# Four convolution channel tiles instead of two during prompt attention, softmax scaling on ScalarE, low parts on VectorE, first steps reordered

## The chip, the cores and the metric

The kernel runs on one core of one Trainium2 chip. The metric is device time in microseconds (us), lower is better. Times of a kernel are medians of several executions; the trace comes from one more execution, taken with the hardware profiler.

Engines are named as in the profile: PE is TensorE (matmuls and transposes), PEld its weight loads, DVE is VectorE, ACT is ScalarE, POOL is GpSimd, SP is SyncE, which issues most transfers. L1108 is line 1108 of the kernel before.

## What is computed

One layer of a hybrid model in fp32, for a prompt of 512 tokens and 8 single-token samples together (520 columns, model width 1024):

```
z = rms_norm(x) @ w_in                 -> u2, q, k/v of three branches, gates
u = u2[:, :1024] * sigmoid(u2[:, 1024:])
c = conv1d(u, 31 taps per channel)     -> layer_norm -> silu -> @ w_conv_pw
a = sparse attention of 16 heads: compressed keys, selected blocks, window;
    each branch: softmax(q.k - slope * distance), times a gate, times v
x = x + (sigmoid(g_conv)*c + sigmoid(g_attn)*a) @ w_out
y = rms_norm(x + relu(rms_norm(x) @ w_up)^2 @ w_down)
```

The prompt attends to itself. The samples attend to paged caches of 2,048 positions in device memory, fetched by gathers. For the prompt, the selected blocks are all blocks, so it has two full branches and a short compressed one.

## The kernel before

**Layout.** Activations lie transposed, channels on the 128 partitions and the 520 columns along the free axis, so the model width is 8 channel tiles. A dense product (`dense`, L433 to L435) takes three fp32r matmuls per 128x128 weight tile, because each fp32 operand is split into a high part (a cast) and a low part (the difference): `hH*wh + hL*wh + hH*wl`. For every 128 output channels `wload` fetches the weights in two halves `wraw` (128x512), casts each on ACT to `wh` (L411) and subtracts for `wl` (L412). Two such `wh`/`wl` pairs exist. L412 runs on `LOW[0]`, which is POOL from the start and `LOW2` from the sample stage on; the third to sixth weight tile and the two large products at the end use DVE.

**Stages.** The order on each engine comes from a planner that simulates the program with priorities, except for the first normalization, whose order is the string `NORDER`.

1. Start (0 to 75 us). `norm1` normalizes five row tiles of x: `q` squares and sums a row tile on ACT, `s` turns sums into factors on DVE and ACT, `m` multiplies by the factor and the gain on DVE (L338), `t` transposes on PE (L346), casts to `hH` on ACT (L348) and subtracts for `hL` on DVE (L349). Then the first q tiles are projected. `small_loads` issues small constants on SP; `small_prep` transposes `vr` and the convolution weights `cwr` with PE (L308). `build_k` makes high and low parts of a head group's keys in one half of the partitions, and a DMA on ACT's queue copies them to the other half (L624).
2. Prompt attention (75 to 455 us). `attend` runs 4 head groups, each with two pairs of heads, each pair with two full branches: 16 units. A unit scores 4 query tiles of two heads (PE L688), adds distances and takes a minimum (DVE L651), exponentiates (ACT L655), scales the probabilities (L739 on DVE for query tiles 1 and 2, L741 on POOL for 0 and 3), transposes them (PE L750), copies them out of PSUM into `pt` (L753, one head on ACT, one on DVE) and multiplies by v (PE L755). Projections of the next group, pooling of the compressed cache (POOL gathers, L317) and the first convolution tiles fill in around it.
3. Convolution. `u_proj` computes the gated channel tile `u` (two buffers, `U1`); `conv_taps` then runs 31 taps per tile on DVE, a first one (L1101) and 30 more (L1108), each reading `u` shifted by one column and the sum `y`. `UP1` and `Y1` = 2 tiles have their `u` and `y` in memory of the prompt stage; the other six need memory that comes free after it. `U_EARLY` says behind which score matmul the PE work of an early `u` is queued, `V_AT` behind which score operation the first later tile's first tap is queued.
4. Sample stage (455 to 660 us). For 10 columns of work, cache rows are gathered, transposed on PE, copied by ACT, scored, exponentiated and weighted (L936 to L953), while the other six convolution tiles run on DVE and gate projections on PE.
5. Transition (660 to 725 us): sample results, convolution norm (L1179, L1182), activation (L1212 to L1219), its split (L1225, L1226), `gate_conv` projections.
6. Merge and output product (725 to 815 us), then the two large products (to 1195 us).

`after(ins)` wraps `tc.issue_after(ins)`. This queues the wrapped instructions behind `ins`, but only those that run on the same engine as `ins`, and it adds no wait between engines.

Of the kernel before, what the change touches and what calls it, by code (L numbers as in the profile page):

```python
# [17 lines left out]
P = 128  # L18
# [14 lines left out]
TL_S = True  # L33
KTS_B, SG_B, U1, Y1, UP1 = 5, 6, 2, 2, 2
SC_D = (1, 2)
PS1 = {"pss": 2, "pst": 2, "pso": 1, "psp": 1}
# [3 lines left out]
SORDER = (8, 9, 0, 1, 2, 3, 4, 5, 6, 7)  # L40
LOW2 = "gpsimd"
CG_B, QK_B = 4, 2
CONV_D = (0, 1, 2, 3, 4, 5, 6, 7)
CONV_S, W_V2 = (), 20
PT_A = (0,)
RT_E = lambda nc: nc.gpsimd
# [9 lines left out]
U_AT, V_AT = 108, 121  # L56
U_EARLY = (32, 48, 0, 0)
POOL_P, PROJ_D = True, False
# [6 lines left out]
SQ_D, WARM, EARLY = (), 20, 2  # L65
NORDER = "q0 s01 q1 m0 s12 m1 t0 t1 q2 q4 q3 s25 m4 m2 t4 m3 t2 t3"
PACK = 5000
# [63 lines left out]
def hybrid_layer(ctx: ExitStack, tc: tile.TileContext, I, C, O):  # L131
# [14 lines left out]
    def f32(ap):  # L146
        return ap.bitcast(F32)
# [124 lines left out]

    def small_loads():
        nc.sync.dma_start(wp, I["cmp_w"][0])
        cw_ = I["cmp_w"]
        for s in range(2):
            nc.sync.dma_start(wq[:, s], bass.AP(tensor=cw_.tensor, offset=cw_.offset + 32 * s, ap=[[0, 32], [8, 4], [1, 8]]))
        nc.sync.dma_start(wqb, bass.AP(tensor=cw_.tensor, offset=cw_.offset + 32, ap=[[0, 8], [2, 16], [1, 2]]))
        for r in range(2):
            nc.sync.dma_start(pos2[:, :, r], I["cmp_pos"][0])  # L280
        for s in range(2):
            nc.sync.dma_start(w1bd[64 * s:64 * s + 64, :, 64 * s:64 * s + 64], I["cmp_w1"][0].rearrange("j d e -> d j e"))
            nc.sync.dma_start(w2bd[64 * s:64 * s + 64, :, 64 * s:64 * s + 64], I["cmp_w2"][0].rearrange("j e f -> e j f"))
        nc.sync.dma_start(dist, C["dist"])
        for i, n in enumerate(("ln2_g", "conv_b", "conv_ln_g", "conv_ln_b")):
            nc.sync.dma_start(vr[8 * i:8 * i + 8], I[n][0].rearrange("(k p) -> k p", p=P))
        nc.sync.dma_start(cwr, I["conv_w"][0])

# [32 lines left out]
    def norm1():  # L321
# [14 lines left out]
        def scale(j):  # L336
            n = P if j < 4 else NB
            dve.scalar_tensor_tensor(xts[j][:n], xts[j][:n], rs[:n, 0, j:j + 1], g1b[:n], op0=OP.mult, op1=OP.mult)  # L338

# [15 lines left out]
        for op in NORDER.split():  # L355
            a = int(op[1])
            if op[0] == "q":
                squares(a)
            elif op[0] == "s":
                stats(slice(a, int(op[2])))  # L360
            elif op[0] == "m":
                scale(a)
            else:
                last = turn(a)
# [14 lines left out]
        return last  # L379

    hH = hp.tile([P, KD, T], F32R, name="hH", tag="H")
    hL = hp.tile([P, KD, T], F32R, name="hL", tag="L")
# [20 lines left out]

    def wload(w, pieces, r0=0, low=None):
        raws = early.pop(pieces[0][0], None) or wfetch(w, pieces, r0)
        o = sum(n for c, n in pieces)
        wh = wts.tile([P, KD, P], F32R, name="wh")
        wl = wts.tile([P, KD, P], F32R, name="wl")
        for h, raw in enumerate(raws):
            a, b = wh[:, KD // 2 * h:KD // 2 * h + KD // 2, :o], wl[:, KD // 2 * h:KD // 2 * h + KD // 2, :o]  # L410
            act.copy(a, raw[:, :, :o])  # L411
            (low or (dve if 2 <= len(loaded) < LOW_D else LOW[0])).tensor_tensor(b, raw[:, :, :o], f32(a), op=OP.subtract)  # L412
        loaded.append(wh)
        return wh, wl

    def after(ins):
        return tc.issue_after(ins.ins) if ins else nullcontext()
# [196 lines left out]
    def build_k(g, r, ap):  # L614
        kt = KV[g][0]
        w = ap.tile([P, 2, NP_ + 32], F32R, name="rt", bufs=RT_B)
        t = RT[g, "k", r] = w[:, :, 32:]
        RT[g, "ck", r] = w
        if r == 1 and g > 0:
            add_ck(g)  # L620
        a, o = 64 * r, 64 - 64 * r
        act.copy(t[a:a + 64, 0], kt[a:a + 64, :NP_])
        dve.tensor_sub(t[a:a + 64, 1], kt[a:a + 64, :NP_], f32(t[a:a + 64, 0]))
        DUP_E(nc).dma_start(f32(t[o:o + 64]), f32(t[a:a + 64]))  # L624

# [3 lines left out]
    def attend(g, ap):  # L629
# [10 lines left out]
        for pr in range(2):  # L640
# [24 lines left out]
            for r in (0, 1, -1):  # L665
# [69 lines left out]
                for e in range(2):  # L735
                    for i in range(4):
                        ph = phs[e][i]
                        if i in SC_D:
                            dve.tensor_scalar(ph, ph, rr[:, e, i:i + 1], None, op0=OP.mult)  # L739
                        else:  # L740
                            pool.tensor_scalar(ph, ph, rr[:, e, i:i + 1], 1.0, op0=OP.mult, op1=OP.mult)  # L741
                for js in ((0,), (1,), (2, 3)):
# [344 lines left out]
    def conv_taps(ks, share):  # L1087
        prev = None
        for k in ks:
# [9 lines left out]
            else:  # L1099
                with after(HV[V_AT] if k == max(UP1, ks[0]) and V_AT else prev):  # L1100
                    dve.tensor_scalar(yk, u[:, 0:NP_], cwT[:, k, 0:1], cbv[:, k:k + 1], op0=OP.mult, op1=OP.add)  # L1101
            for w in range(1, CW):
# [229 lines left out]
    with tc.manual_schedule():  # L1332
        last = norm1()
    ready = [wload(w_in, [(C_Q + P * t, P)]) for t in range(2)]
    small_loads()
# [308 lines left out]
```

## Time and profile before

| | |
|---|---|
| median of 3 runs | 1199.42 us (1198.84 to 1204.34) |
| profiled execution, its own time | 1196.95 us |
| span in the trace, first to last instruction | 1195.18 us, 1.77 us less than its own time |
| mean granted TensorE clock | 0.981 of full speed |
| busy in the span | PE 94%, PEld 86%, DVE 65%, ACT 47%, POOL 32% |

Busy means that an instruction is in the engine. Matmuls overlap, and their ends are modelled, so PE can be 100% busy below its peak rate. An engine's idle time in a stretch is the length of the stretch minus its busy time. The granted clock is 1.0 at 2.4 GHz and 0.5 at 1.2 GHz. Times in rows count from the start of the span.

### The profile page before, as it was taken

The numbers are of one execution on the slowest core, as the hardware profiler recorded it, in microseconds if no ns is written. First come the engines' busy times: TensorE is split into PE (matmuls) and PEld (weight loads), VectorE is DVE, ScalarE is ACT, GpSimd is POOL, SyncE is SP. The second block draws the span as 40 slices with busy tenths as digits, with TensorE's granted clock in tenths as the row PEclk, the third lists the DMA queues.
The fourth block names the chain that finished last, engine by engine and source line by source line (L and its number), as shares of the span: only waits on it lengthen the run. The fifth ranks groups of instructions, "written<-read, shape, count | busy, mean of one in ns | idle before, by whom it ended". The sixth has DMA issues, their size and how long they took to land.

```text
span 1195.2 us, 24820 instructions
## 1 busy us (share of the span) xinstructions
PE 1126.9 (94%) x9755; PEld 1025.3 (86%) x9755; DVE 773.2 (65%) x1712; ACT 557.1 (47%) x1404; POOL 385.2 (32%) x378
## 2 busy tenths in 40 slices
PE   6899999998999999989889979999999999999996
PEld 6787976876776888878777769999999999999996
DVE  6442566595977868999998886456543443443476
ACT  5453477545667544445444454344431441431454
POOL 2435637545652333545553334440000000000012
PEclk8899999999999999999999889999999999999999
DMA  6645654564468417867774233333333333333354
GB/s 180 196 137 165 191 168 118 158 175 150 116 185 298 133 38 274 279 241 250 252 253 169 64 105 108 89 89 107 89 96 100 89 89 89 95 99 90 89 164 138
DMA packets 189037, 176.78 MB, mean 148 GB/s; under 512 B 35309, under 2 KB 171053, under 8 KB 183656
## 3 DMA queue, kind: packets, MB, share of 16 engines
q1 hardware_dynamic: 172472, 96.54, 28.5%
q0 software_dynamic: 15296, 76.55, 18.2%
q10 hardware_dynamic: 1152, 2.10, 0.8%
q8 instruction: 77, 1.26, 0.4%
q14 instruction: 40, 0.33, 0.1%
HBM read 167.58 MB, written 14.80 MB: 153 GB/s over the span
## 4 chain that ended last, share of the span: by engine, by line
PE 71%; DVE 20%; DMA 4%; issue 2%; SPq 1%; ACT 1%; POOL 1%; DVEq 0%; POOLq 0%; ACTq 0%
PE psd L433 18%; PE psd L435 17%; PE psd L434 17%; DVE y L1108 13%; PE pss L688 4%; PE pst L750 3%; PE pso L755 3%; PE psp L783 2%; DMA wraw<-in_w_in_dram 1%; DMA cg<-in_cache_cmp_kv_dram,gic 1%; DVE tq L943 1%; DVE y L1212 1%; DMA rt<-rt 1%; PE pso L729 1%; PE psp L790 1%
## 5 line engine op out<-in xcount | busy, mean ns | idle before, releaser
L411 ACT CAST wh<-wraw 128x512 fp32r<-128x512 f32 x282 | 161.7, 617 | 266.9 <-PE psd L434 201.8
L433 PE MATMUL psd<-hH,wh 128*128 128x256 f32 (+2 forms) x848 | 248.3, 295 | 2.2 <-ACT gc L1249 1.3
L435 PE MATMUL psd<-hH,wl 128*128 128x256 f32 (+2 forms) x848 | 247.1, 294 | 0.1
L434 PE MATMUL psd<-hL,wh 128*128 128x256 f32 (+2 forms) x848 | 245.7, 291 | 0.0
L412 POOL TENSOR_TENSOR wl<-wraw,wh 128x512 fp32r<-128x512 f32 x130 | 180.7, 1409 | 199.5 <-ACT wh L411 188.3
L1108 DVE SCALAR_TENSOR_TENSOR y<-u,cwT,y 128x512 f32<-128x512 f32 x240 | 221.7, 924 | 6.0
L433 PEld LDWEIGHTS psd<-hH,wh 128*128 128x128 f32 (+1 forms) x848 | 160.7, 190 | 7.6 <-issue 2.5
L435 PEld LDWEIGHTS psd<-hH,wl 128*128 128x128 f32 (+1 forms) x848 | 160.4, 190 | 4.3 <-issue 2.8
L434 PEld LDWEIGHTS psd<-hL,wh 128*128 128x128 f32 (+1 forms) x848 | 160.8, 190 | 1.8 <-issue 0.7
L433 PE MATMUL psd<-xgH,wh 128*128 128x264 f32 (+1 forms) x512 | 144.8, 283 | 0.0
L434 PE MATMUL psd<-aT,wh 128*128 128x264 f32 (+1 forms) x512 | 144.7, 283 | 0.0
L433 PE MATMUL psd<-aT,wh 128*128 128x264 f32 (+1 forms) x512 | 144.7, 283 | 0.0
L435 PE MATMUL psd<-aT,wl 128*128 128x264 f32 (+1 forms) x512 | 144.7, 283 | 0.0
L435 PE MATMUL psd<-xgH,wl 128*128 128x264 f32 (+1 forms) x512 | 144.5, 282 | 0.0
L412 DVE TENSOR_TENSOR wl<-wraw,wh 128x512 fp32r<-128x512 f32 x152 | 103.9, 723 | 62.5 <-ACT wh L411 59.3
L434 PE MATMUL psd<-xgL,wh 128*128 128x264 f32 (+1 forms) x512 | 144.2, 282 | 0.0
L1583 POOL TENSOR_TENSOR attnT<-attnT,gfb 128x512 f32<-128x512 f32 (+1 forms) x8 | 10.5, 1331 | 368.7 <-DVE sqd L1578 368.7
L434 PEld LDWEIGHTS psd<-xgL,wh 128*128 128x128 f32 x512 | 96.6, 189 | 0.0
L655 ACT ACTIVATE pp<-pp,st 128x256 f32<-128x256 f32 (+3 forms) x128 | 71.6, 559 | 53.7 <-DVE st L651 52.1
L435 PEld LDWEIGHTS psd<-xgH,wl 128*128 128x128 f32 x512 | 96.5, 188 | 0.0
L433 PEld LDWEIGHTS psd<-aT,wh 128*128 128x128 f32 x512 | 96.3, 188 | 0.1
L433 PEld LDWEIGHTS psd<-xgH,wh 128*128 128x128 f32 x512 | 96.3, 188 | 0.0
(378 smaller groups left out, 2326.3 us busy)
## 6 DMA issues: line engine op xcount, KB each, us to landing
wraw<-in_w_in_dram SPq DMA_DIRECT2D x88, 256.0 KB
wraw<-in_w_down_dram SPq DMA_DIRECT2D x80, 256.0 KB
wraw<-in_w_up_dram SPq DMA_DIRECT2D x64, 256.0 KB
sg<-in_state_win_kv_dram POOLq DMA_DIRECT2D x8, 1024.0 KB
out_dram<-in_state_win_kv_dram SPq DMA_DIRECT2D x8, 1022.0 KB
wraw<-in_w_in_dram SPq DMA_DIRECT2D x32, 128.0 KB
wraw<-in_w_conv_pw_dram SPq DMA_DIRECT2D x16, 256.0 KB
wraw<-in_w_out_dram SPq DMA_DIRECT2D x16, 256.0 KB
```

The costliest lines, as they stand in the source:

```text
L411: act.copy(a, raw[:, :, :o])
L412: (low or (dve if 2 <= len(loaded) < LOW_D else LOW[0])).tensor_tensor(b, raw[:, :, :o], f32(a), op=OP.subtract)
L433: pe.matmul(ps[:n], wh[:, k, :n], aH[:, k, c], start=(k == 0), stop=False)
L434: pe.matmul(ps[:n], wh[:, k, :n], aL[:, k, c], start=False, stop=False)
L435: end = pe.matmul(ps[:n], wl[:, k, :n], aH[:, k, c], start=False, stop=(k == KD - 1))
L655: act.activation(ph, ph, AF.Exp, scale=-1.0, bias=st[:, 0, e, i:i + 1], accum_out=st[:, 1, e, i:i + 1])
L688: hpe = pe.matmul(ps, rq[:, e, P * i:P * i + P], kk[:, l, 32 - xi:32 + nk], start=(l == 0), stop=(l == 1))
L729: packed([lambda i=i, e=e: pe.matmul(po[64 * e:64 * e + 64, P * i:P * i + P], VcZ[:, i], pt[:, e], start=False, stop=True, skip_group_chec ...
L750: pe.transpose(ps[:, o:o + P], phs[e][i][:, P * j:P * j + P], ident)
L755: packed([lambda j=j, e=e: pe.matmul(po[64 * e:64 * e + 64, P * j:], vt[:, j, r], pts[e][:, off[j]:off[j] + P * (4 - j)], start=(r == 0 an ...
L783: packed([lambda r=r, j=j, i=i: pe.matmul(po[32 * i:32 * i + 32, j], wpa[:, 2 * rh + r, j], gs[i][:, r, 256 * j:256 * j + 256], start=(rh ...
L1108: prev = dve.scalar_tensor_tensor(yk, u[:, w:w + NP_], cwT[:, k, w:w + 1], yk, op0=OP.mult, op1=OP.add)
```

## The change

- `UP1` and `Y1` go from 2 to 4: four channel tiles have their `u` and `y` in the prompt stage, and `U_EARLY` queues the PE work of the third and fourth behind score matmuls 56 and 74 of 128. `U1` stays 2.
- The probabilities of all four query tiles are scaled on ACT (an activation `Copy` with a per-partition scale) instead of on DVE and POOL, and both `pt` copies run on ACT (`PT_A`).
- A tile's first tap runs on ACT instead of DVE.
- `LOW2` becomes DVE: from the sample stage on, L412 leaves POOL.
- Start: both sums before the factors (`q0 q1 s02`), tile 0 and 1 multiplied one after the other; `after(scaled[1])` around L412 of the first two weight tiles; `vr` and `cwr` are loaded first among the small loads; for head group 0, ACT and DVE write the second half of the keys instead of a DMA.
- The scratch memory for descriptors of POOL's transfers is set to 8192 bytes per partition, half of the default.

```diff
-KTS_B, SG_B, U1, Y1, UP1 = 5, 6, 2, 2, 2
-SC_D = (1, 2)
+KTS_B, SG_B, U1, Y1, UP1 = 5, 6, 2, 4, 4
-LOW2 = "gpsimd"
+LOW2 = "vector"
-PT_A = (0,)
+PT_A = (0, 1)
-U_EARLY = (32, 48, 0, 0)
+U_EARLY = (32, 48, 56, 74)
-NORDER = "q0 s01 q1 m0 s12 m1 t0 t1 q2 q4 q3 s25 m4 m2 t4 m3 t2 t3"
+NORDER = "q0 q1 s02 m0 m1 t0 t1 q2 q4 q3 s25 m4 m2 t4 m3 t2 t3"
...
     def small_loads():
+        nc.sync.dma_start(cwr, I["conv_w"][0])
+        for i, n in enumerate(("ln2_g", "conv_b", "conv_ln_g", "conv_ln_b")):
+            nc.sync.dma_start(vr[8 * i:8 * i + 8], I[n][0].rearrange("(k p) -> k p", p=P))
         nc.sync.dma_start(wp, I["cmp_w"][0])
...
-        for i, n in enumerate(("ln2_g", "conv_b", "conv_ln_g", "conv_ln_b")):
-            nc.sync.dma_start(vr[8 * i:8 * i + 8], I[n][0].rearrange("(k p) -> k p", p=P))
-        nc.sync.dma_start(cwr, I["conv_w"][0])
...
-                scale(a)
+                scaled.append(scale(a))
...
-    def wload(w, pieces, r0=0, low=None):
+    def wload(w, pieces, r0=0, low=None, ins=None):
...
-            (low or (dve if 2 <= len(loaded) < LOW_D else LOW[0])).tensor_tensor(b, raw[:, :, :o], f32(a), op=OP.subtract)
+            with after(ins):
+                (low or (dve if 2 <= len(loaded) < LOW_D else LOW[0])).tensor_tensor(b, raw[:, :, :o], f32(a), op=OP.subtract)
...
+        if g == 0:
+            act.copy(t[o:o + 64, 0], kt[a:a + 64, :NP_])
+            dve.tensor_sub(t[o:o + 64, 1], kt[a:a + 64, :NP_], f32(t[a:a + 64, 0]))
+            return
         DUP_E(nc).dma_start(f32(t[o:o + 64]), f32(t[a:a + 64]))
...
-                        if i in SC_D:
-                            dve.tensor_scalar(ph, ph, rr[:, e, i:i + 1], None, op0=OP.mult)
-                        else:
-                            pool.tensor_scalar(ph, ph, rr[:, e, i:i + 1], 1.0, op0=OP.mult, op1=OP.mult)
+                        act.activation(ph, ph, AF.Copy, scale=rr[:, e, i:i + 1])
...
-                    dve.tensor_scalar(yk, u[:, 0:NP_], cwT[:, k, 0:1], cbv[:, k:k + 1], op0=OP.mult, op1=OP.add)
+                    act.activation(yk, u[:, 0:NP_], AF.Identity, scale=cwT[:, k, 0:1], bias=cbv[:, k:k + 1])
...
-    ready = [wload(w_in, [(C_Q + P * t, P)]) for t in range(2)]
+    ready = [wload(w_in, [(C_Q + P * t, P)], ins=scaled[1]) for t in range(2)]
...
-    nc = bacc.Bacc("TRN2", target_bir_lowering=False, num_devices=1)
+    nc = bacc.Bacc("TRN2", target_bir_lowering=False, num_devices=1, dynamic_dma_scratch_size=8192)
```

## Rows read from the trace of the kernel before

**Rows 1.** The page: the chain that ended last, shares by engine.

```profile
PE 71%; DVE 20%; DMA 4%; issue 2%; SPq 1%; ACT 1%; POOL 1%; DVEq 0%; POOLq 0%; ACTq 0%
```

**Rows 2.** By stage: length, busy PE, PEld, DVE, ACT, POOL (instructions), clock, DMA, GB/s.

```profile
75.00:455.00 380.00, 366.36 (x3028) 300.31 (x3027) 250.19 (x757) 213.22 (x658) 191.61 (x211) 1.00 0.54 160
159.00:236.00 77.00, 73.38 (x595) 59.37 (x595) 47.88 (x188) 53.00 (x178) 41.28 (x51) 1.00 0.48 138
455.00:660.00 205.00, 186.10 (x1984) 162.86 (x1982) 194.31 (x268) 100.99 (x231) 97.97 (x87) 0.98 0.69 241
660.00:725.00 65.00, 53.84 (x461) 48.17 (x460) 53.49 (x122) 30.90 (x57) 17.52 (x13) 0.89 0.30 82
725.00:815.00 90.00, 90.00 (x756) 89.84 (x756) 49.18 (x83) 37.15 (x73) 40.71 (x28) 1.00 0.36 106
```

**Rows 3.** DVE's costliest group, sample stage: busy us, mean ns, idle before.

```profile
L1108 DVE SCALAR_TENSOR_TENSOR y<-u,cwT,y 128x512 f32<-128x512 f32 x176 | 163.3, 928 | 4.9
```

**Rows 4.** The same line, whole span: shortest, median and longest in ns.

```profile
L1108 DVE SCALAR_TENSOR_TENSOR y<-u,cwT,y x240: 729/752/3104, 239.1 to 652.3; 128x512 f32<-128x512 f32 x120
```

**Rows 5.** Line L412, whole span: shortest, median and longest in ns.

```profile
L412 DVE TENSOR_TENSOR wl<-wraw,wh x152: 347/689/1787, 37.1 to 1179.9; 128x512 fp32r<-128x512 f32 x150, 128x192 fp32r<-128x192 f32 x2
L412 POOL TENSOR_TENSOR wl<-wraw,wh x130: 1252/1297/2504, 9.6 to 800.9; 128x512 fp32r<-128x512 f32 x130
```

**Rows 6.** Line L412 by stage: DVE busy, POOL busy, clock, DMA.

```profile
455.00:660.00 205.00, 0.00 (x0) 45.84 (x33) 0.98 0.69 241
660.00:725.00 65.00, 0.00 (x0) 17.52 (x13) 0.89 0.30 82
```

**Rows 7.** The chain that ended last, transition: start us, us, what.

```profile
694.54 8.73 DVE y L1212 x7
```

**Rows 8.** POOL by line, prompt attention.

```profile
L741 POOL TENSOR_SCALAR pp<-pp,st 128x128 f32<-128x128 f32 x64 | 39.4, 631 | 58.3 <-DVE st L661 28.9 <-DVE st L662 21.0 <-ACT pc L655 8.1
```

**Rows 9.** DVE by line, prompt attention.

```profile
L739 DVE TENSOR_SCALAR pp<-pp,st 128x256 f32<-128x256 f32 x64 | 31.4, 544 | 0.3
L753 DVE COPY pt<-pst 128x384 f32<-128x384 f32 (+1 forms) x48 | 28.7, 598 | 39.1 <-PE pst L750 36.1 <-PE pss L688 1.5 <-ACT pp L655 0.8
```

**Rows 10.** ACT by line and shape, whole span; the page's row for L655.

```profile
L655 ACT ACTIVATE pp<-pp,st 128x256 f32<-128x256 f32 (+3 forms) x128 | 71.6, 559 | 53.7 <-DVE st L651 52.1
L753 ACT COPY pt<-pst 128x384 f32<-128x384 f32 x32 | 15.2, 474 | 22.0 <-PE pst L750 20.3 <-PE pss L697 0.7 <-PE pss L688 0.7
L753 ACT COPY pt<-pst 128x512 f32<-128x512 f32 x16 | 9.3, 579 | 8.1 <-PE pst L750 8.0
```

**Rows 11.** PE by line, prompt attention: what ended its idle time.

```profile
L750 PE MATMUL pst<-ident,pp 128*128 128x128 f32 x320 | 55.7, 284 | 5.9 <-POOL pp L741 4.0 <-DVE news L598 1.6 <-ACT pt L753 0.3
```

**Rows 12.** Line L741 by stretch: POOL busy (instructions).

```profile
159.00:236.00 77.00, 11.43 (x20) 1.00 0.48 138
```

**Rows 13.** Timeline of the start: start us, us, engine, line, what [idle before].

```profile
7.81 1.28 DVE L338 SCALAR_TENSOR_TENSOR xt<-xt,rs,g1b 128x1024 f32<-128x1024 f32 x1 [0.76 <-DMA g1b<-in_ln_g_dram]
9.57 4.93 POOL L412 TENSOR_TENSOR wl<-wraw,wh 128x512 fp32r<-128x512 f32 x4 [7.25 <-ACT wh L411]
13.34 2.25 DVE L338 SCALAR_TENSOR_TENSOR xt<-xt,rs,g1b 128x1024 f32<-128x1024 f32 x1
15.64 1.97 PE L346 MATMUL pss<-ident,xt 128*128 128x128 f32 x8 [5.40 <-DVE xt L338]
17.43 0.80 PE L433 MATMUL psd<-hH,wh 128*128 128x256 f32 x2
31.32 0.65 PE L308 MATMUL pst<-ident,cwr 31*128 31x31 f32 x8 [2.56 <-DMA cwr<-in_conv_w_dram]
57.68 1.41 PE L688 MATMUL pss<-rt 128*128 128x128 f32 x4 [3.01 <-DMA rt<-rt]
```

**Rows 14.** The clock in the start.

```profile
33.00:36.00 3.00, 3.00 (x17) 3.00 (x16) 2.86 (x19) 0.00 (x0) 1.34 (x2) 0.52 0.01 3
58.00:63.00 5.00, 5.00 (x24) 4.57 (x24) 1.99 (x6) 1.21 (x4) 0.25 (x1) 0.50 1.04 327
```

More of the change, by code (lines that the diff above doesn't have):

```diff
@@ L337, in scale @@
             n = P if j < 4 else NB
-            dve.scalar_tensor_tensor(xts[j][:n], xts[j][:n], rs[:n, 0, j:j + 1], g1b[:n], op0=OP.mult, op1=OP.mult)
+            return dve.scalar_tensor_tensor(xts[j][:n], xts[j][:n], rs[:n, 0, j:j + 1], g1b[:n], op0=OP.mult, op1=OP.mult)
         def turn(j):
@@ L379, in norm1 @@
         return last
+    scaled = []
     hH = hp.tile([P, KD, T], F32R, name="hH", tag="H")
```

## Prediction

> **What bounds the kernel now.** I read the chain of waits first, then busy time by stage, then the lines inside the stages that the diff touches. PE holds 71% of the chain and DVE 20% [rows 1], so the stages differ. In prompt attention PE is busy 366.4 of 380 us [rows 2] and idles 13.6. In the sample stage DVE is the full engine, 194.3 of 205 us, and PE idles 18.9 us; most of that DVE time is convolution taps, 163.3 us [rows 2, 3]. In the transition PE idles 11.2 of 65 us at a clock of 0.89, while DVE is busy 53.5. From 725 to 815 us PE has no idle time, so only work on PE itself could matter there. The time to win is 30 us of PE idle time between 455 and 725 us, and the holes of the start.
>
> **Taps.** Two channel tiles move forward: 60 taps by 0.928 us, the sample stage's mean [rows 3], is 55.7 us off DVE there and on DVE in prompt attention. With the median of 0.752 [rows 4] it would be 45.1. The `u` projections of these tiles are the same PE work at an earlier place. With them move 8 weight transfers on SP, 8 casts on ACT and 8 subtractions on POOL, 1.3 us each [rows 5]; POOL has room, 191.6 of 380 us busy [rows 2] less what it loses below. They cost nothing in sum; if PE waited for those weights, at most their own PE work, some 23 us (192 matmuls by 366.4/3028 us), would stand still.
>
> **Low parts.** 33 subtractions leave POOL in the sample stage [rows 6] and come to DVE at 0.689 us each [rows 5]: plus 22.7 us. They also stop colliding. The median tap takes 0.752 and the longest 3.104 us [rows 4]. A similar instruction, L338, took 1.28 us alone and 2.25 us while POOL ran four of these subtractions [rows 13]. If all of the excess of the remaining 116 taps (0.928 less 0.752) is POOL's, 20.4 us come back; if none, nothing. I take 15, since L412 is the largest part of POOL's tensor work there. DVE after: 194.3 - 55.7 + 22.7 - 15 = 146 us. PE with 186 us then sets the stage: **minus 19** (bounds 0 and 19; busy PE time is itself stretched by waits, so somewhat more is open). In the transition 13 more come to DVE [rows 6], 9.0 us against 11.5 us of idle DVE time, thin cover, worth 9 us if it fails. From 725 to 815 us, 28 are hidden by PE, with DVE at 49.2 + 19.3 of 90 us [rows 2].
>
> **Transition.** Taps now end last in the sample stage. With 40 us of DVE slack they end well before the last sample column, and the convolution norm starts inside the stage. Its seven L1212 instructions on the chain take 1.25 us each [rows 7] beside POOL's subtractions, which leave. I take all of PE's idle time, **minus 11** (bounds 0, and 17 if the clock is also full: 11% of 53.8 us).
>
> **Softmax work on ACT.** DVE loses 31.4 + 28.7 us and POOL 39.4 [rows 8, 9]. DVE in the prompt ends at 250.2 + 55.7 - 60.1 = 246 us, no fuller than now. No row has the scaling on ACT. From below: the `pt` copies grow by 0.82 ns a column [rows 10], which at the mean width of 320 columns is 0.42 us, 54 us for 128. From above: the exponentials of the same tiles, 71.6 us [rows 10]. These read the same memory and take a per-partition operand too, so I take 70. The copies cost 9.3 + 15.2 us on ACT, as their twins do [rows 10], and four first taps about 3. ACT goes from 213.2 to 311 of 380 us, 82%.
>
> What of this is on the path? Per unit, POOL's 2.46 us of scaling (DVE's 1.96 beside it) become 4.4 us, and copies that ran two at a time, 1.79 us at the longest, become 3.06 in a row: plus 3.2 us in each of 16 units, 51 us. PE has other work meanwhile. Now it idles 4.3 us before the transposes for scaling and copies [rows 11], of 68 us that POOL's scaling and DVE's copies take: 6%. Of 51 us that would be 3. With ACT so much fuller I take three times that: **plus 10** (bounds minus 13.6, all of PE's idle time gone because more filler is at hand, and plus 51).
>
> The Trainium skill (ScalarE: Activation LUTs, Rules for kernel authors) says to put multiplications on VectorE, not ScalarE. By its figures (What ACT_TABLE_LOAD costs: 186 ns plus 0.833 ns a column, and 93 ns for a pointer operand) an estimate for the 128 scalings is 70 us, and by the sum above nothing would change; no run so far shows such a scaling on ACT.
>
> **Start.** Now the second row tile's multiplication ends at 15.59 us, PE idles 5.40 us before its transposes, and the first projection starts at 17.43 [rows 13]. With one factor chain for three tiles the first multiplication starts some 0.8 us later than 7.81 (an estimate) and the second follows directly. The new `after(scaled[1])` holds nothing: `scaled[1]` is DVE's, these subtractions are POOL's, and only instructions of the same engine are queued. So they still collide and I take 1.28 and 2.25 us: 12.1 us, minus 3.5 (minus 4.4 without collision). PE's wait of 2.56 us for `cwr` goes, as `cwr` is issued several transfers earlier; with it most of a stretch at a clock of 0.52, the 1.2 GHz level, after PE had idled (33 to 36 us, worth 1.4) [rows 14]. Queued behind it now are `wp` and `pos`, which PE needs just before; they come five small issues later on SP. The wait of 3.01 us for the copy of the keys goes [rows 13], and with it 5 us at a clock of 0.50 right behind that wait, worth 2.5 [rows 14]. In its place are two casts and two subtractions on ACT and DVE, about 1 us on the path. What is late next is the projections' weights, since transfers ran at full share then (1.04). Sum 3.5 + 2.56 + 1.4 + 3.01 + 2.5 - 1, **minus 12** (bounds 6, the first two alone, and 17, if the rest of the start also stays at 2.4 GHz).
>
> **Priced at nothing.** The first taps lose their queue order (they are ACT's now), which only frees the planner. The smaller descriptor scratch: the trace shows no full ring; at worst gathers hold as much again as all transfers do on the chain, 4% or 48 us [rows 1].
>
> **Sum.** -12 + 10 - 19 - 11 = -32 on the span of 1195.2 us: 1163.2, or 1165 as the profiled execution's own time (1.77 us more). The median before is 2.5 us above that execution, so **1167**.
>
> **Rivals.**
> ACT becomes the bound of prompt attention. For: in the stretch from 159 to 236 us ACT is busy 53.0 of 77 us [rows 2] with 5 units (20 of 64 scalings) [rows 12]. Each gets 98/16 = 6.1 us more, 83.5 in all, so the stretch grows by 6.5 us even with ACT full, and by 16 with ACT at 90%. Over 16 units that is 21 to 50 us in place of 10. Against: the mean of 82%, and units are spread over 380 us with gaps for projections. Time 1178 to 1207, middle 1192. The rule of the Trainium skill quoted above speaks for this one.
>
> Slower: the heads are a serial chain and ACT takes instructions in order, so the full 51 us land on the path, and more where a scaling stands behind casts that wait for a weight buffer. 1199.4 - 42 + 51 = 1208, up to 1259 if the queue doubles it. It decides against the change once over 48 us land, 3 us a unit. Against: PE's filler hides 94% of the present waits.
>
> The sample stage isn't set by DVE: the taps stand in the chain, but a column's own sequence or its gathers end as late. 1199.4 - 12 + 10 = 1197, no change. Against: a DMA share of 0.69, which becomes 0.76 at 186 us, and DVE's 95%.
>
> More than forecast: DVE's and POOL's relief also closes half of PE's holes in the prompt (7), start 17, later stages 36: 1139.
>
> **How the numbers follow.** Forecast 0.60 (1155 to 1180), ACT as bound 0.14, slower 0.06, sample stage not set by DVE 0.06, more 0.14 (1139 to 1155). Within 0.5% is 1193.4 to 1205.4, about what a measurement can tell from no change. Faster: 0.60 + 0.14 + 0.09 of the ACT case = 0.83; same: 0.04 of it + 0.06 = 0.10; slower: 0.01 of it + 0.06 = 0.07. The range of 1148 to 1197 leaves out half of "more" and all that is slower, 0.14.
>
> **What will show it.** Right: first projection near 14 us, no PE wait for `cwr` or the key copy; DVE well below 95% in the sample stage, taps near 0.76 us, PE idle there under 5 us; `y` norm instructions before the last sample column; ACT near 80% in the prompt. Wrong: PE idle before L750 growing to tens of us with ACT as releaser, a prompt stage longer by over 20 us, taps that still end last, or POOL waiting for transfers before gathers.

## The result, and the profile after

The changed kernel takes 1208.59 us (median of 8 runs, 1202.92 to 1210.18), the kernel before beside it 1199.13. The ratio is **1.0068, 95% interval 1.0043 to 1.0094**: slower by some 8 us, where 32 us less were forecast, and outside the range. Its profiled execution has a span of 1201.0 us, 5.8 more than before. Ratios here and below leave out three disturbed executions, one each of e1, e9 and e25, that took 1563 to 2184 us.

I cut both spans at the first score matmul, the last copy of an attention result and the first instruction of the merge. The windows (length, busy PE, PEld, DVE, ACT, POOL with instructions, clock, DMA share, GB/s), of before with these bounds:

```profile
0.00:57.70 57.70, 43.14 (x325) 39.98 (x325) 30.10 (x84) 27.54 (x58) 19.54 (x28) 0.91 0.65 183
57.70:452.30 394.60, 380.95 (x3127) 312.59 (x3128) 255.68 (x777) 219.28 (x676) 195.74 (x213) 0.99 0.53 158
452.30:723.90 271.60, 241.54 (x2456) 212.50 (x2455) 246.74 (x385) 131.88 (x288) 116.19 (x100) 0.96 0.60 206
723.90:1195.00 471.10, 461.26 (x3853) 460.24 (x3851) 240.71 (x466) 178.37 (x383) 53.77 (x38) 0.99 0.34 102
```

and of after:

```profile
0.00:49.80 49.80, 39.17 (x290) 36.22 (x291) 26.88 (x77) 24.29 (x52) 16.50 (x25) 0.93 0.61 175
49.80:510.90 461.10, 428.22 (x3404) 350.36 (x3403) 274.73 (x774) 310.30 (x888) 155.72 (x149) 0.96 0.50 149
510.90:725.40 214.50, 203.06 (x2181) 175.96 (x2180) 151.83 (x323) 125.19 (x269) 50.77 (x54) 0.96 0.68 235
725.40:1201.00 475.60, 465.48 (x3887) 464.46 (x3885) 246.42 (x494) 177.40 (x381) 12.87 (x10) 0.99 0.35 102
```

The stages moved by -7.9, +66.5, -57.1 and +4.3 us (the last window of before ends 0.2 us short of its span). About half of that is PE's work changing its place: prompt attention has 277 PE instructions more, the sample stage 275 fewer, the start 35 fewer and the end 34 more. What moves are dense products, which the last stage of before runs at 471.1/3853 = 0.122 us an instruction. So I take 0.122 us for each instruction off a difference of length and call the rest the stage's **own** loss or gain. For prompt attention it is 66.5 - 277 x 0.122 = 32.6 us. The others are -3.6 (start), -23.5 (sample stage with transition) and +0.1 (end).

So the start gave 3.6 where 12 were forecast, the sample stage and the transition 23.5 of 30, and prompt attention took 32.6 in place of 10.

What answers to [rows 1], [rows 4] and [rows 5] in the profile after (the chain by engine; taps and low parts, shortest, median and longest in ns):

```profile
PE 77%; DVE 11%; DMA 6%; ACT 3%; issue 2%; SPq 1%; POOL 0%; DVEq 0%; ACTq 0%; POOLq 0%
...
L1110 DVE SCALAR_TENSOR_TENSOR y<-u,cwT,y x240: 695/747/3085, 258.4 to 601.7; 128x512 f32<-128x512 f32 x120
...
L413 POOL TENSOR_TENSOR wl<-wraw,wh x52: 1268/1291/2265, 9.6 to 375.8; 128x512 fp32r<-128x512 f32 x52
```

DVE's share of the chain fell from 20% to 11%. The taps end at 602 us, not 653, and DVE is busy 151.8 of 214.5 us in the sample stage: it no longer sets that stage, as forecast. The taps of the stage, for [rows 3], and those that now run in prompt attention:

```profile
L1110 DVE SCALAR_TENSOR_TENSOR y<-u,cwT,y 128x512 f32<-128x512 f32 x91 | 64.6, 753 | 0.5 <-ACT y L1103 0.2
...
L1110 DVE SCALAR_TENSOR_TENSOR y<-u,cwT,y 128x512 f32<-128x512 f32 x150 | 125.2, 850 | 4.4 <-ACT y L1103 2.7
```

In the sample stage, where POOL no longer subtracts, a tap takes 753 ns. The 850 ns of prompt attention are a mean of two parts: the 85 taps up to 376 us, while POOL still subtracts, take 907 ns, the 65 after it, beside a single subtraction, 775.

ACT in prompt attention, by line, for [rows 8 to 10]:

```profile
L660 ACT ACTIVATE pp<-pp,st 128x128 f32<-128x128 f32 (+3 forms) x128 | 71.6, 560 | 22.0 <-DVE st L656 18.6 <-issue 2.8
L743 ACT ACTIVATE pp<-pp,st 128x128 f32<-128x128 f32 (+3 forms) x128 | 59.8, 551 | 10.6 <-DVE st L667 10.5
L755 ACT COPY pt<-pst 128x384 f32<-128x384 f32 (+1 forms) x96 | 47.5, 509 | 49.5 <-PE pst L752 47.3 <-PE pss L702 1.5 <-issue 0.3
```

The scaling takes 59.8 us, between the bounds of 54 and 71.6, and ACT's busy time of 310.3 us is near the forecast 311 (317 with the window of before cut as here). The work was priced rightly; what it does to the path was not. PE's waits in prompt attention, after (what PE waited for: us in total, times, longest); in the kernel before its longest entry is 4.0 us:

```profile
PE psp L785 <- DMA cg<-in_cache_cmp_kv_dram,gic: 7.9, 5, 3.4
PE pst L731 <- ACT pt L755: 7.8, 3, 4.1
PE pss L693 <- DVE st L656: 6.1, 10, 1.5
PE pso L757 <- ACT pt L755: 2.7, 2, 2.4
PE psd L434 <- ACT ga L1239: 2.4, 1, 2.4
```

PE idles 461.1 - 428.2 = 32.9 us there, before 394.6 - 381.0 = 13.6: 19.3 us more. The other 13.3 of the 32.6 are longer busy time for the same work, and the clock, 0.96 after 0.99, is large enough for it: with levels of 1.0 and 0.5, that is 8% of 461 us at 1.2 GHz against 2% of 395, 29 us more, which cost at most half, 14.5 (an estimate from rounded clocks).

One stretch shows how it can come about. From the timeline of after (start us, us, engine, line, what, idle before), and last the same matmuls at another place, from the chain of waits:

```profile
182.59 0.95 POOL L316 DMA_INDIRECT cg<-in_cache_cmp_kv_dram,gic  x1 [20.00 <-PE psp L785]
...
185.95 1.08 PE L757 MATMUL pso<-pt,qkv 128*64 128x512 f32 x4 [2.36 <-ACT pt L755]
...
186.31 3.73 ACT L743 ACTIVATE pp<-pp,st 128x128 f32<-128x128 f32 x8
...
192.74 3.64 PE L785 MATMUL psp<-cg,wpa 128*32 128x256 f32 x32 [3.29 <-DMA cg<-in_cache_cmp_kv_dram,gic]
...
201.17 0.48 ACT L755 COPY pt<-pst 128x384 f32<-128x384 f32 x1 [8.21 <-PE pst L752]
...
150.30 1.86 PE psp L785 x32
```

and the clock there:

```profile
175.00:200.00 25.00, 18.70 (x140) 11.82 (x138) 5.99 (x31) 17.88 (x52) 11.11 (x11) 0.82 0.44 127
192.70:196.40 3.70, 3.66 (x33) 1.66 (x33) 0.00 (x0) 0.26 (x2) 1.27 (x1) 0.50 0.32 68
```

ACT works without a pause from 168 to 192.9 us, and two groups of eight scalings, 3.72 and 3.73 us, stand in that row. PE waits 2.36 us for a copy. Then it stands 3.29 us behind a gather, with the next transposes queued after it. The gathers that it waits for start only at 182.59 us, since POOL had waited 20.00 us for PE's previous pooling matmuls. The pooling matmuls that follow run at the lower level: 3.64 us, 1.86 elsewhere. ACT, whose next instruction is a copy of those transposes, idles 8.21 us. Each engine is late for the other in turn, which busy shares of a whole stage don't show. This is one stretch; that the other losses come about in the same way is not shown.

The start, for [rows 13] and [rows 14] (timeline, then windows):

```profile
8.38 3.59 DVE L337 SCALAR_TENSOR_TENSOR xt<-xt,rs,g1b 128x1024 f32<-128x1024 f32 x2
9.61 5.98 POOL L413 TENSOR_TENSOR wl<-wraw,wh 128x512 fp32r<-128x512 f32 x4 [7.29 <-ACT wh L411]
13.69 0.50 PE L434 MATMUL psd<-hH,wh 128*128 128x256 f32 x2 [0.57 <-ACT hH L347]
27.56 0.98 PE L299 MATMUL pst<-wp,pos 32*128 32x1 f32 x4 [3.53 <-DMA pos<-in_cmp_pos_dram]
```

```profile
26.00:30.00 4.00, 2.34 (x14) 2.17 (x15) 1.42 (x7) 0.93 (x3) 0.00 (x0) 0.66 0.41 102
30.00:34.00 4.00, 4.00 (x19) 4.00 (x20) 3.93 (x24) 0.00 (x0) 0.55 (x1) 0.50 0.07 19
```

The first projection starts at 13.69 us instead of 17.43, the forecast 3.5 earlier. POOL's subtractions still collide with the two multiplications (3.59 us): the wrapper around them orders nothing, and e9, which leaves it out, starts its first projection at 13.63 us. The wait for `cwr` became one of 3.53 us for `pos`, which is now queued behind it, and the stretch at half clock stayed.

### The profile page after: what moved, and what is told of

Same layout as the page of the kernel before. It is cut to its first block, busy times and chain, and to the rows that moved or that the text cites. A ratio compares the mean times of both kernels' runs of the same rounds, so it can differ in the third digit from the quotient of the medians.

```text
span 1201.0 us, 24795 instructions
## 1 busy us (share of the span) xinstructions
PE 1135.9 (95%) x9755; PEld 1027.0 (86%) x9755; DVE 699.9 (58%) x1666; ACT 637.2 (53%) x1589; POOL 235.9 (20%) x236
## 4 chain that ended last, share of the span: by engine, by line
PE 77%; DVE 11%; DMA 6%; ACT 3%; issue 2%; SPq 1%; POOL 0%; DVEq 0%; ACTq 0%; POOLq 0%
PE psd L434 19%; PE psd L436 19%; PE psd L435 19%; DVE y L1110 6%; DMA cg<-in_cache_cmp_kv_dram,gic 3%; PE pss L693 3%; PE pso L757 3%; PE psx L938 3%; PE pst L752 2%; PE psp L785 2%; PE psy L942 1%; PE psy L952 1%; DMA sg<-in_cache_slc_kv_dram,gix 1%; DVE pp L656 1%; ACT pp L743 1%
## 5 line engine op out<-in xcount | busy, mean ns | idle before, releaser
L436 PE MATMUL psd<-hH,wl 128*128 128x264 f32 (+2 forms) x848 | 243.1, 289 | 0.0
L413 DVE TENSOR_TENSOR wl<-wraw,wh 128x512 fp32r<-128x512 f32 (+1 forms) x230 | 156.9, 718 | 82.3 <-ACT wh L411 78.1
L1110 DVE SCALAR_TENSOR_TENSOR y<-u,cwT,y 128x512 f32<-128x512 f32 x240 | 189.0, 813 | 4.9 <-ACT y L1103 2.9
L656 DVE CUSTOM_DVE_ANT_0 pp<-pss,dist 128x128 f32<-128x128 f32 (+3 forms) x128 | 61.1, 486 | 80.1 <-PE pss L693 53.4
L434 PEld LDWEIGHTS psd<-aT,wh 128*128 128x128 f32 x512 | 96.3, 188 | 0.1
L435 PEld LDWEIGHTS psd<-aT,wh 128*128 128x128 f32 x512 | 96.2, 188 | 0.0
```

Of the source, the lines that this page charges most:

```text
L434: pe.matmul(ps[:n], wh[:, k, :n], aH[:, k, c], start=(k == 0), stop=False)
L435: pe.matmul(ps[:n], wh[:, k, :n], aL[:, k, c], start=False, stop=False)
L436: end = pe.matmul(ps[:n], wl[:, k, :n], aH[:, k, c], start=False, stop=(k == KD - 1))
L656: v = dve.tensor_tensor_reduce(out=ph, in0=ps, in1=bias, scale=slope[e], scalar=FLOOR, op0=OP.add, op1=OP.min, accum_out=st[:, 0, e, i:i + 1])
L1110: prev = dve.scalar_tensor_tensor(yk, u[:, w:w + NP_], cwT[:, k, w:w + 1], yk, op0=OP.mult, op1=OP.add)
```

## The experiments

Eighteen kernels. The table gives the ratio to before, the four cuts in us, and each stage's own change against before as worked out above (start, prompt attention, sample stage with transition). Cuts are of one profiled execution each. That of after and that of e21 lie over 5 us below the median of their kernel, and 19 executions of before alone spread from 1193.17 to 1205.17 us.

| kernel | ratio, 95% interval | first score, last result, merge, end | own changes |
|---|---|---|---|
| before | 1 | 57.7, 452.3, 723.9, 1195.2 | 0, 0, 0 |
| after | 1.0068 [1.0043, 1.0094] | 49.8, 510.9, 725.4, 1201.0 | -3.6, +32.6, -23.5 |
| e2_soft_only | 1.0282 [1.0240, 1.0324] | 57.5, 486.3, 759.9, 1227.4 | -0.2, +31.6, -1.4 |
| e10_scale_only | 1.0138 [1.0090, 1.0187] | 58.3, 469.0, 741.5, 1212.7 | +0.7, +21.4, -4.5 |
| e11_pt_only | 1.0007 [0.9992, 1.0021] | 57.5, 450.1, 717.1, 1191.6 | -0.2, +1.5, -5.1 |
| e4_taps_only | 1.0125 [1.0087, 1.0164] | 58.4, 503.7, 738.0, 1213.4 | +0.7, +17.7, -0.1 |
| e12_no_taps | 1.0055 [1.0030, 1.0081] | 58.0, 493.3, 726.8, 1201.5 | +0.3, +8.5, -2.5 |
| e22_scratch | 0.9979 [0.9955, 1.0002] | 59.2, 464.3, 717.8, 1193.5 | +1.5, +4.5, -7.8 |
| e5_low_only | 0.9994 [0.9975, 1.0012] | 57.6, 454.5, 729.5, 1196.5 | 0, +2.9, -3.1 |
| e6_taps_low | 0.9980 [0.9953, 1.0007] | 57.4, 498.4, 714.5, 1190.3 | -0.2, +13.5, -18.1 |
| e9_start_only | 1.0016 [0.9994, 1.0037] | 49.5, 454.5, 726.7, 1198.2 | -3.8, +5.8, +0.7 |
| e16_pace | 0.9974 [0.9954, 0.9993] | 60.2, 454.3, 723.7, 1192.8 | +2.5, -0.5, -4.4 |
| e1_soft_off | 0.9969 [0.9953, 0.9985] | 51.2, 498.8, 713.4, 1189.1 | -2.1, +10.2, -14.6 |
| e21_pt_kept | 1.0051 [1.0031, 1.0071] | 48.5, 498.7, 722.7, 1198.6 | -4.9, +17.6, -9.6 |
| e3_taps_off | 1.0025 [1.0009, 1.0042] | 51.8, 476.8, 719.1, 1197.2 | -1.6, +25.8, -22.1 |
| e17_soft_low | 1.0109 [1.0081, 1.0137] | 58.4, 488.4, 741.0, 1208.0 | +0.7, +33.3, -22.8 |
| e18_soft_tap | 1.0271 [1.0233, 1.0308] | 56.7, 484.0, 751.9, 1230.6 | -0.9, +35.0, +0.9 |
| e13_three | 0.9904 [0.9886, 0.9921] | 51.4, 481.1, 705.7, 1181.7 | -2.0, +5.4, -17.3 |
| e24_three_old_start | 0.9878 [0.9851, 0.9906] | 57.5, 483.2, 705.2, 1180.7 | -0.2, +5.8, -20.0 |
| e25_three_late | 0.9913 [0.9883, 0.9944] | 49.2, 477.9, 703.1, 1179.1 | -4.2, +8.5, -21.0 |

**What an order alone is worth** (e16, e22). One pace weight 56 to 57; and the scratch alone:

```diff
-PRI_C, PRI_S, PRI_V, W_V = 2000, 500, 100, 56
+PRI_C, PRI_S, PRI_V, W_V = 2000, 500, 100, 57
```

```diff
-    nc = bacc.Bacc("TRN2", target_bir_lowering=False, num_devices=1)
+    nc = bacc.Bacc("TRN2", target_bir_lowering=False, num_devices=1, dynamic_dma_scratch_size=8192)
```

> Before with one planner weight, the pace of the taps, set to 57 instead of 56 (same instructions, another order from the prompt on): a control of what a new order alone does to the time. Theory (an order is worth a few us either way): 1194 to 1204. Rival (the order of before is a lucky one): 1205 to 1215.

> Before with only the smaller descriptor scratch. Theory (gathers don't need it; only the order of the prompt shifts a little): 1192 to 1203. Rival (gathers wait for descriptors, which is part of what four tiles cost with it): 1204 to 1216.

The first theories are the nearer ones (1193.71 us for e16, 0.3 below its range). A new order from the planner (e16) moves the total by 3 us and one stage by 4.4, the scratch (e22) the total by 2.5 and one stage by 7.8. This is the grain of the table: single own changes of a few us mean nothing. No cost of the scratch can be told from it.

**Softmax work, on the kernel before** (e2, e10, e11):

```diff
-                        if i in SC_D:
-                            dve.tensor_scalar(ph, ph, rr[:, e, i:i + 1], None, op0=OP.mult)
-                        else:
-                            pool.tensor_scalar(ph, ph, rr[:, e, i:i + 1], 1.0, op0=OP.mult, op1=OP.mult)
+                        act.activation(ph, ph, AF.Copy, scale=rr[:, e, i:i + 1])
...
-PT_A = (0,)
+PT_A = (0, 1)
```

e2 has both hunks, e10 the first, e11 the second.

> The kernel before with the softmax work on ScalarE and nothing else of the change. Theory (ScalarE's added work lengthens prompt attention): the last attention result moves from 452 to 480 us or later and the time rises to 1215 to 1245 us, since no tap moves out of the sample stage in return. Rival (the moved taps do it): within 6 us of the kernel before.

> Before with only the scaling of probabilities on ScalarE; one of the two copies out of PSUM stays on VectorE. Together they cost 34 us. Theory (the scaling carries it, 4 us in a row per unit on an engine that also has the exponentials): prompt attention 20 to 30 us longer, time 1215 to 1228. Rival (the two copies in a row carry it, since TensorE waits for them directly): 1196 to 1206.

> Before with only both copies out of PSUM on ScalarE; the scaling stays on VectorE and GpSimd. Scaling alone cost 15 us, both together 34. Theory (the two add, since both stand in a row on ScalarE in each unit): prompt attention 15 to 20 us longer, 1212 to 1222. Rival (the copies cost only beside the scaling, when ScalarE's queue is already long): 0 to 6 us longer, 1197 to 1206.

The theory of e2 held, 34 us. In e10 its interval is 9 to 19 per mille, its median of 1214.16 just under the 1215 expected; in e11 the rival is the nearer one, 1195.96 us, 1 below its range. Scaling alone costs 15 to 17 us, copies alone nothing, both 34: here the copies cost only beside the scaling. Prompt attention of e2:

```profile
57.50:486.30 428.80, 396.57 (x3148) 319.94 (x3149) 203.75 (x664) 294.90 (x856) 154.50 (x149) 0.96 0.49 145
```

PE idles 32.2 us at a clock of 0.96, the same two signs as after, without any tap moved. ACT is only 69% busy.

**Four tiles** (e4, e12):

```diff
-KTS_B, SG_B, U1, Y1, UP1 = 5, 6, 2, 2, 2
+KTS_B, SG_B, U1, Y1, UP1 = 5, 6, 2, 4, 4
...
-U_EARLY = (32, 48, 0, 0)
+U_EARLY = (32, 48, 56, 74)
```

with the smaller scratch. e12 is e4 and leaves out taps:

```diff
-            for w in range(1, CW):
+            for w in range(1, 1 if k in (2, 3) else CW):
```

> The kernel before with four channel tiles in prompt attention (and the smaller descriptor scratch that makes room for them) and nothing else. Theory (only ScalarE's added work lengthens the prompt): the prompt ends by 470 us, the sample stage and transition shrink by 25 us or more, time 1175 to 1190. Rival (the moved taps lengthen the prompt): its end moves by 30 us or more and the time is 1195 to 1215.

> The kernel with four channel tiles in prompt attention and nothing else changed, but with 30 taps of the third and of the fourth tile left out (60 taps, part of the convolution is not computed); their projections stay in prompt attention. Theory (60 taps on VectorE hold up the scores' additions and with them the heads): prompt attention ends some 20 us earlier than with the taps (503.7 us there), time 1190 to 1198. Rival (the moved projections and what they wait for make the prompt longer, the taps hide): end of prompt attention 498 to 506 us, time 1208 to 1216.

My theory of e4 fell: four tiles alone are slower by 15 us. Prompt attention has 270 PE instructions more (33 us) and loses 17.7 beside them; the sample stage gives back what left it and nothing else. Without the 60 taps prompt attention's own loss is 8.5, so e12 lies between its theory and its rival: about half of the loss is the taps (PE's waits for DVE's additions to the scores fall from 6.8 to some 3 us), half comes with the projections and the smaller scratch, whose own change of 4.5 (e22) is within the grain. Why the sample stage gained nothing is suggested by the chain of waits of e4, there (start us, us, what):

```profile
637.04 2.50 POOL wl L412 x2
...
641.68 6.14 DMA sg<-in_cache_slc_kv_dram,gix
```

POOL's low parts stand in front of its gathers. The next edit takes them away, but with them also their collisions with the taps, so that the two aren't told apart.

**Low parts on DVE** (e5 alone, e6 with four tiles):

```diff
-LOW2 = "gpsimd"
+LOW2 = "vector"
```

> Before with only the low parts on VectorE from the sample stage on. Theory (VectorE sets the sample stage of the kernel before, and its taps collide with GpSimd's subtractions): 22.7 us come to VectorE and up to 20 us of stretched taps come back, median tap near 0.75 us; the two nearly cancel, time 1190 to 1205. Rival (the collisions, and GpSimd's own delays of gathers, are worth more than the moved work): 1175 to 1190. Second rival (VectorE only gets fuller): 1205 to 1220.

> As the run with four channel tiles alone, and the low parts of the weights on VectorE from the sample stage on. Theory: the taps run at 0.75 us there instead of about 0.9, VectorE ends earlier, 5 to 12 us faster than that run: 1168 to 1183. Rival (the sample stage is then set by TensorE, so this brings nothing): within 4 us of that run.

e5: the two halves cancel as its first theory said. DVE by line in its sample stage, for [rows 3]:

```profile
L1108 DVE SCALAR_TENSOR_TENSOR y<-u,cwT,y 128x512 f32<-128x512 f32 x180 | 138.1, 767 | 4.1
L412 DVE TENSOR_TENSOR wl<-wraw,wh 128x512 fp32r<-128x512 f32 x44 | 30.7, 706 | 17.4 <-ACT wh L411 17.3
```

180 taps take 138.1 us where 176 took 163.3, and 30.7 us of low parts come. With four tiles, where DVE has room, the same edit is worth 19 us (1212.79 to 1193.41), more than the 5 to 12 expected, though the time itself is above the range.

**The start alone** (e9): the three edits of the start (`NORDER`, `small_loads`, `build_k`; without the wrapper).

> Before with only the edits of the start (order of the first normalization, small loads first, second half of the first keys written by ScalarE and VectorE). Theory (what is won before the first score reaches the end): first score 6 to 8 us earlier, time 1188 to 1191. Rival (the prompt attention gives it back, because its weights and gathers arrive no earlier): first score as early, time 1194 to 1199.

The rival is the nearer one, at 1200.90 us even beyond its range. The first score comes 8.2 us earlier, but 36 PE instructions (4.4 us) have only moved behind it, and what is left of 3.8 us is lost in prompt attention, within the grain: its second pair of heads ends at 200 us, before at 197.

**The changed kernel with one part taken back** (e1: softmax work as before; e21: scaling as before; e3: two tiles), with the diffs above reversed.

> The changed kernel with the softmax work back where it was: scaling on VectorE and GpSimd, the second copy of the transposed probabilities on VectorE. Theory (ScalarE's added work lengthens prompt attention): the last attention result, at 510 us in the changed kernel, comes at 455 to 475 us, the gain of the sample stage stays, and the time is 1165 to 1180 us. Rival (the two moved convolution tiles lengthen it through VectorE): the prompt still ends at 495 us or later and the time stays at 1195 to 1215, or more, because VectorE has the softmax work as well.

> The changed kernel with only the scaling back on VectorE and GpSimd; both copies out of PSUM stay on ScalarE. With copies back too it was 16 us faster than the changed kernel. Theory (copies alone cost nothing, scaling is the cost): 1188 to 1197. Rival (VectorE, which now has 60 taps more, gains from being rid of the copies): 1178 to 1188. Second rival (they cost beside the taps): 1198 to 1206.

> The changed kernel with two channel tiles in prompt attention instead of four (the second pair of places in the order taken back too); softmax work on ScalarE, low parts on VectorE and the start stay changed. Theory (parts add up: softmax work plus 34 us, low parts alone nothing, start alone nothing): 1225 to 1237, slower than the changed kernel. Rival (the four tiles are what makes the changed kernel slow, as they alone cost 15 us): 1190 to 1200.

e1 falls between its two cases: the softmax work costs some 12 us in the changed kernel (1.0068 against 0.9969), not 34 and not all that is lost. Prompt attention alone loses 22 us by it, 15 of them by the scaling and 7 by the copies (e21); the sample stage then comes out 9 to 14 us shorter, for reasons that stay open. In the totals it is the other way round: of the 12 us the copies cost 10 and the scaling 2 (e21, 1.0051), which speaks for e21's second rival and against its theory. e3 is the miss that I can't sum from parts: 1.0025, in the range of its rival, where the parts sum to over 30 us. It also says what the two more tiles are worth in the changed kernel: with them it is 5 us slower, and the sample stage's own gain is 22.1 us without them, 23.5 with them.

**Why e3 is so cheap** (e17: e2 with low parts on DVE; e18: e2 with first taps on ACT).

> Before with the softmax work on ScalarE and the low parts on VectorE. Softmax work alone costs 34 us, low parts alone nothing, but the changed kernel with two tiles, which has both, the new start and the first taps on ScalarE, costs only 3 us. Theory (with VectorE relieved in prompt attention its taps start earlier and the low parts then fit beside them, so these two together give most of the 31 us back): 1200 to 1212. Rival (the low parts do nothing here either): 1224 to 1236.

> Before with the softmax work and the first tap of each tile on ScalarE. Theory (the first tap on VectorE stands in its queue behind the next tile's product, which waits for ScalarE, so the taps start 30 us late; on ScalarE it starts as soon as its tile is there): taps of the third tile start 20 to 30 us before prompt attention ends, time 1200 to 1215. Rival (the order of the taps doesn't matter, VectorE is full later anyway): 1224 to 1236.

e17 gives 20 of the 31 us back (1.0282 to 1.0109; 1214.1 us, just outside the range of its theory), all in the sample stage and the transition; but its taps start at 489.6 us, no earlier, so the reason that I gave for it is wrong. e18 gives nothing. The remaining 10 us or so between e17 and e3 were not separated.

**Better than both** (e13: e1 with three tiles; e24: the same without the edits of the start; e25: e13, its third tile behind score matmul 80):

```diff
-KTS_B, SG_B, U1, Y1, UP1 = 5, 6, 2, 4, 4
+KTS_B, SG_B, U1, Y1, UP1 = 5, 6, 2, 3, 3
...
-U_EARLY = (32, 48, 56, 74)
+U_EARLY = (32, 48, 56, 0)
```

> The changed kernel with the softmax work back on VectorE and GpSimd, and three channel tiles in prompt attention instead of four. Theory (with the low parts on VectorE and four tiles, VectorE runs out of taps some 115 us before the sample stage ends, so the fourth tile is better left there): prompt attention ends 20 to 28 us earlier than with four (498.8 us), the sample stage is 12 to 18 us longer, time 1180 to 1188. Rival (VectorE sets the sample stage again and it gives back all): 1190 to 1198.

> Three channel tiles in prompt attention, low parts on VectorE, first taps on ScalarE, smaller scratch, on the kernel before; softmax work and the start stay as before. With the new start this was 11.4 us faster than before. Theory (the start's earlier first score is lost in prompt attention here too): 1181 to 1189, the same as with the new start. Rival (with the sample stage relieved, the start's gain arrives): 1190 to 1195.

> The version with three tiles (new start, softmax work as before), its third tile's TensorE work queued behind score matmul 80 instead of 56. Theory (between 56 and 80 the heads' scores stand behind the third tile; later there is as much room, so nothing changes beyond an order's few us): 1180 to 1190. Rival (later is better, as the heads then end sooner): 1170 to 1179.

The first theories held by their times; for e13 prompt attention ends 17.7 us earlier than in e1 and the sample stage is 10 longer, both a little less than expected. The lowest time is that of e24, 1181.83 us against 1197.69, 1.2% under before: the softmax work and the start as before, three tiles, low parts on DVE, first taps on ACT, the smaller scratch. Its stages:

```profile
57.50:483.20 425.70, 409.29 (x3334) 340.01 (x3335) 304.72 (x857) 231.22 (x699) 184.59 (x204) 0.98 0.52 157
483.20:705.20 222.00, 209.89 (x2214) 179.79 (x2214) 170.95 (x352) 127.49 (x275) 54.57 (x55) 0.96 0.67 231
```

Prompt attention's own loss is 5.8 us and the sample stage's gain 20. Old and new start, early and late third tile agree within their intervals. The fourth tile costs 8 us (e1 against e13).

## Why the prediction was wrong

**Where it failed, by stage and by edit.** By stage the largest miss is prompt attention, 32.6 us for plus 10. By edit it is the moved tiles. Taken back from the changed kernel, the softmax work is worth 12 us in all (e1), near the 10 booked, while the two tiles, which with the low parts were to bring the minus 19 and minus 11, cost 5 (e3), and the start brings nothing (e9). The two accounts differ because the edits act on each other: what an edit takes in prompt attention, another stage gives back in part.

**Softmax work on ACT: the step that failed in its stage.** "PE has other work meanwhile": I took the 6% of the present waits that reach PE and made three times that of the new ones, plus 10. Alone the edit costs 34 us (e2). In the changed kernel prompt attention loses 32.6 in all, some 22 of them by this edit (after against e1); that 9 of these come back in the sample stage, so that 12 are left, was not forecast, and that this is near 10 is luck. The present share was no guide. In the stretch shown above, ACT's row of work and PE's row wait for each other, work queued behind the waiting instruction waits too, and the clock is at 0.50 after it; that this is the reason throughout is argued. Of the rivals, ACT as bound (21 to 50 us) is the nearer one in size. ACT is full only for short stretches, 19.9 of 20 us from 170 us and 19.1 from 210, and 67% busy over the stage. "Slower" has nearly the measured time, 1208, but by 51 us on the path and full gains of 42, and neither came.

The rule of the Trainium skill (ScalarE: Activation LUTs, Rules for kernel authors) came out right in e10, which puts only those multiplications on ACT and is 1.4% slower. The reason that it gives, DVE's speed per element in bf16, was not at work: DVE's scalings took 544 ns on average [rows 9], ACT's 551. The estimate of 70 us by the Trainium skill (ScalarE: Activation LUTs, What ACT_TABLE_LOAD costs) left out that by the same section back-to-back activations overlap by some 93 ns. With that the estimate by this section is 58 us, and the trace has 59.8.

**The sign to look for was wrong as well.** I expected the waits before the transposes L750. Those fell to 0.5 us, from 5.9 [rows 11]; the waits for ACT's copies show at the transposes of the compressed branch (L731, 7.8 us) and at products (L757, 2.7), others at gathers further along.

**Taps: priced at nothing in prompt attention.** This step failed too. That they "cost nothing in sum" is false: four tiles alone lose 17.7 us there (e4), about half by the taps (e12). I had counted DVE's busy time (246 us of 380), not that the scores' additions queue behind taps. In the changed kernel this is smaller, since e1 loses 10.2 with everything but the softmax work, and four tiles against two cost 6.8 (after against e3).

**Sample stage and transition: near in number, not shown in cause.** Forecast 30, measured 23.5, with DVE at 71%, taps at 753 ns and the norm inside the stage (it starts at 610 us, and PE works on sample columns until 707). But I booked the gain to the taps that leave, and e3 has 22.1 of it without moving them, e17 22.8 with only the softmax work and the low parts. On the kernel before, four tiles alone gain nothing there (e4), low parts alone neither (e5), both 18.1 (e6). So the low parts have to leave POOL and something else has to change as well; why the softmax work serves for that as well as the tiles do stays open.

**Start: the credit wrong, and one local term.** 3.5 us at the first projection came, and the key copy's wait went, with the clock at 1.00 behind it. The 2.56 + 1.4 for `cwr` did not come: its wait became that for `pos`, 3.53 us, with 4 us at a clock of 0.50. But I booked the first score's earlier start as a gain at the end. Of 7.9 us 4.3 are work put off, and alone the edits change nothing that can be told (e9), nor with three tiles (e13 against e24).

**The sum.** Against the forecast the start misses 8.4 us, prompt attention 22.6, and the sample stage 6.5: 37.5. With the forecast of -32 that is +5.5, and the measured +5.8 but for rounding and the end.

**The chances.** I gave 0.07 to slower, nearly all of it to the case that the whole 51 us land. 22.6 us more than forecast in prompt attention were enough, because the gains shrank by 15 as well.

## What to carry to other kernels

Before booking a stage's gain, count the bottleneck engine's instructions in each stage on both sides: over half of the 57 us that the sample stage lost here, 33.6 us, was work that prompt attention got. Work moved between two queues that wait for each other isn't priced by busy shares or by today's waits; time the one edit alone, as e10 did. An edit's price also depends on the others (the softmax work: 34 us alone, 12 in the changed kernel), and two edits that bring nothing to a stage singly can do so together (e4, e5, e6), so take parts back from the whole as well as adding them to the start.

## What the runs showed that I had not expected

A stall can cost twice: after PE's wait of 3.29 us behind a gather the next 32 matmuls took 3.64 us instead of 1.86 at a granted clock of 0.50. The same taps take 753 ns where POOL gathers but doesn't subtract (sample stage of after), 907 beside its subtractions in prompt attention and 928 in the sample stage of before. And a planner's order moves a single stage by 4.4 us (e16), the smaller scratch one by 7.8 (e22), without a change of work.
